# Sixteen modulation pieces multiplied in the loop over the Hyena filter jobs

## The chip, the cores and the metric

The kernel runs on one core of a Trainium2 chip. The metric is the device time of one execution in microseconds (us). TensorE (PE) multiplies matrices and loads weights beside that (PEld); VectorE (DVE), ScalarE (ACT) and GpSimd (POOL) compute on tiles; SyncE (SP) issues DMAs. Each engine works off its own instructions in order.

## The reference

A two-layer backbone over 1024 latent tokens of width 1024 and 256 context tokens. Layer 0 mixes tokens with a bidirectional RG-LRU (512 channels) and with an order-2 Hyena (512 channels); layer 1 is a convolution module; each layer ends in a mixture of 16 experts, and each sub-layer is modulated by a vector that depends on the conditioning `c`:

```python
def _adaln(cvec, w_mod, b_mod, n_chunks):
    m = jax.nn.silu(cvec) @ w_mod[:, :n_chunks * D_MODEL] + b_mod[:n_chunks * D_MODEL]
    return [m[:, None, j * D_MODEL:(j + 1) * D_MODEL] for j in range(n_chunks)]

# Hyena in layer 0: kf is the transform of learned filters
kf = _hyena_filters_fft(h.shape[1], p)
z = v
for o in range(HYENA_ORDER):
    z = gates[o] * _fftconv(z, kf[:, o], p['filt_bias'][o])
```

`w_mod` has 1024 x 6144 numbers for each of the two layers; everything is fp32.

## The kernel before, in words

**Modulation.** The product with `w_mod` is cut into pieces. A piece is 128 rows (index k, 0 to 7) by 2048 columns (a third s of a layer's 6144): `ada_load` (L224) takes a buffer of the pool `wr` (tag `w`, four buffers of 1 MB) and issues one 1 MB DMA on SP; `ada_mm` (L235) multiplies it by the conditioning in four matmuls of 128x512, each into its own 32 rows of one PSUM tile, which is held over the eight pieces of a third. After the eighth, `ada_end` copies the sums (L260, ACT), transposes them (L264, four, PE), adds the bias (DVE) and, for s of 1 and 2, transposes two results into rows (L284, PE) and stores them (L287, SP). `fill(n)` does n times: multiply the oldest loaded piece, then load another. 40 pieces are on the list: layer 0 with s = 0, 1, 2 and layer 1 with s = 0, 1. The last third of layer 1 comes later in the kernel and isn't touched.

**Filter stage, 0 to 128 us.** The eight pieces of s = 0 of layer 0 are multiplied at its start, since the norm of x needs them. Then `filters` does eight jobs (four blocks of 128 channels, two orders). A job makes its signal (L413 PE, L414 DVE) one job ahead, transforms it on PE (q0 L436, qa L440/L441, qb L445/L446, 128x128 matmuls), copies sums from PSUM (L455 to L457, ACT), combines them on DVE into K (L458 to L474) and stores K to memory (`kd`, L475, SP). K takes a buffer of the same pool `wr`. Between jobs `next(other)` advances the norm of x (L305 loads, L310, L326 transposes, L329).

**Projections and RG-LRU, 128 to 270 us.** `piece` loads 512 KB of `w_in` (`wst`, L715, SP), splits it into `wh` (L161, ACT) and the remainder `wlo` (L162, DVE), and `proj` multiplies in three passes (L156 to L158, PE, into P).

**Hyena, 270 to 550 us.** Four rounds i, one for each block of 128 channels, two orders each. A round: projection and short convolution of v (`short`, L786 to L788), transform on PE (`hy_fwd` L612, copies L615 on ACT), first step on DVE (`hy_st1` L622/L623), the transform's rest and the product with K on DVE (`hy_mid`, L584 to L640), inverse transform on PE (`hy_inv` L651), gate on DVE (`hy_gate` L659) and transposes back (`to_tok` L668). K is loaded again from `kd` into a buffer of `wr` (L606). In each round `fill(4)` stands before the first transform and again before the second gate's projection, 32 pieces in the four rounds.

**Order.** The program is written as above, and a scheduler then fixes the order of each engine's instructions; SP's DMAs stand in one order too, and one that waits holds up those behind it. So a call that is moved in the text moves others.

**After 550 us** come the output projection, the experts and layer 1.

Of the kernel before, what the change touches and what calls it, by code (L numbers as in the profile page):

```python
# [148 lines left out]
class Builder:  # L149
# [247 lines left out]
    def filters(self, fk, other):  # L397
        nc, A = self.nc, self.A
        V = nc.vector
        c = math.sqrt(0.5)  # L400
        G, Gn, h2, ws = self.G, self.Gn, self.h2, self.ws

        def signal(qd, o):
            cs = slice(qd * 128, qd * 128 + 128)
            if o == 0 and qd + 1 < 4:
                self.filt_win(fk, qd + 1)
            win = self.wins[qd]
            sd = fk.tile([128, 2, 8, 128], F32, name="sd", tag="sd", bufs=2)
            for i in range(2):
                for a in range(0, 8, 4):  # L410
                    q = self.ps.tile([128, 4, 128], F32, name="q", tag="n")
                    for j in range(4):
                        nc.tensor.matmul(q[:, j], h2[:, a + j], ws[:, o, i, cs], start=True, stop=True)  # L413
                    V.tensor_tensor(sd[:, i, a:a + 4], q, win[:, a:a + 4], op=OP.mult)  # L414
            V.tensor_tensor(sd[:1, 0, 0], sd[:1, 0, 0], sd[:1, 1, 0], op=OP.add)
            V.scalar_tensor_tensor(sd[:1, 0, 0], sd[:1, 0, 0], 0.5, self.fbias[:, o, cs], op0=OP.mult, op1=OP.add)
            return sd

        jobs = [(qd, o) for qd in range(4) for o in range(2)]
        sds = [signal(*jobs[0])]  # L420
        for n, (qd, o) in enumerate(jobs):
            sd = sds.pop(0)
            if 0 < n < 7:
                sds.append(signal(*jobs[n + 1]))
            if n:
                for _ in range(3):
                    next(other, None)
            K = self.wr.tile([128, 8, 2, 128], F32, name="w", tag="w")
            q0 = self.ps.tile([128, 2, 2, 128], F32, name="q0", tag="n")
            qa = self.ps.tile([128, 4, 2, 128], F32, name="qa", tag="w")  # L430
            qb = self.ps.tile([128, 4, 2, 128], F32, name="qb", tag="w")
            for i in range(2):
                mc = slice(i * 128, i * 128 + 128)
                oc = slice(128 - i * 128, 256 - i * 128)
                for j, a in enumerate((0, 4)):
                    nc.tensor.matmul(q0[:, j, i], G[:, a, mc], sd[:, i, a], start=True, stop=True)  # L436
            for a in range(1, 4):
                for i in range(2):
                    mc = slice(i * 128, i * 128 + 128)
                    nc.tensor.matmul(qa[:, a, i], G[:, a, mc], sd[:, i, a], start=True, stop=False)  # L440
                    nc.tensor.matmul(qa[:, a, i], G[:, 8 - a, mc], sd[:, i, 8 - a], start=False, stop=True)  # L441
            for a in range(1, 4):
                for i in range(2):
                    oc = slice(128 - i * 128, 256 - i * 128)
                    nc.tensor.matmul(qb[:, a, i], G[:, a, oc], sd[:, i, a], start=True, stop=False)  # L445
                    nc.tensor.matmul(qb[:, a, i], Gn[:, 3 - a, oc], sd[:, i, 8 - a], start=False, stop=True)  # L446
            if n == 0:
                sds.append(signal(*jobs[1]))
                for _ in range(3):
                    next(other, None)  # L450
            T = fk.tile([128, 10, 2, 128], F32, name="kT", tag="kT", bufs=1)
            r4, r1, r2, r3, i1, i2, e0, e4, f, g = (T[:, j] for j in range(10))
            CS = fk.tile([128, 2, 3, 2, 128], F32, name="kC", tag="kC", bufs=1)
            C, S = CS[:, 0], CS[:, 1]
            nc.scalar.copy(r4, q0[:, 1])  # L455
            nc.scalar.copy(T[:, 1:4], qa[:, 1:4])
            nc.scalar.copy(T[:, 4:6], qb[:, 1:3])  # L457
            V.tensor_tensor(e0, q0[:, 0], r4, op=OP.add)  # L458
            V.tensor_tensor(e4, q0[:, 0], r4, op=OP.subtract)
            V.tensor_tensor(f, r1, r3, op=OP.add)  # L460
            V.tensor_tensor(g, r1, r3, op=OP.subtract)
            V.tensor_tensor(C[:, 1], e0, r2, op=OP.subtract)
            V.tensor_tensor(e0, e0, r2, op=OP.add)
            V.tensor_tensor(K[:, 0], e0, f, op=OP.add)
            V.tensor_tensor(K[:, 4], e0, f, op=OP.subtract)
            V.scalar_tensor_tensor(C[:, 0], g, c, e4, op0=OP.mult, op1=OP.add)
            V.scalar_tensor_tensor(C[:, 2], g, -c, e4, op0=OP.mult, op1=OP.add)
            V.tensor_tensor(S[:, 1], i1, qb[:, 3], op=OP.subtract)
            V.tensor_tensor(f, i1, qb[:, 3], op=OP.add)
            V.scalar_tensor_tensor(S[:, 0], f, c, i2, op0=OP.mult, op1=OP.add)  # L470
            V.scalar_tensor_tensor(S[:, 2], f, c, i2, op0=OP.mult, op1=OP.subtract)
            for i, (pl, mi) in enumerate(((OP.add, OP.subtract), (OP.subtract, OP.add))):
                V.tensor_tensor(K[:, 1:4, i], C[:, :, i], S[:, :, i], op=pl)
                V.tensor_tensor(K[:, 7:4:-1, i], C[:, :, i], S[:, :, i], op=mi)  # L474
            nc.sync.dma_start(self.kd[o][qd], K)  # L475

# [126 lines left out]
    def hy_fwd(self, p, J):  # L603
        nc = self.nc
        J["K"] = K = self.wr.tile([128, 8, 2, 128], F32, name="w", tag="w")
        nc.sync.dma_start(K, self.kd[J["o"]][J["qd"]])  # L606
# [64 lines left out]
    def even_mixer(self, st, so):  # L671
        nc, tc, A = self.nc, self.tc, self.A

        def pool(st, name, side=None):
            return st.enter_context(tc.tile_pool(name=name, bufs=1, side=side, reuse_waits="tile"))
# [3 lines left out]
        with ExitStack() as s1, ExitStack() as sl:  # L679
# [4 lines left out]
            with ExitStack() as s2:  # L684
                pf = pool(s2, "fl", "right")
                with tc.tile_pool(name="fs", bufs=1, side="right", reuse_waits="tile") as fs:
                    self.filt_mlp(pf, fs)
                fk = pool(s2, "fk", "right")
                pn = pool(s2, "pn0", "right")
                for _ in range(4):  # L690
                    self.ada_load()
                self.filt_open(fk)
                for k in range(4):
                    self.ada_mm()
                    self.ada_load()

                def halves():
                    for k in range(4):
                        self.ada_mm()
                        if k % 2:  # L700
                            yield
                    rows = [self.norm_rows(pn, A["x"][0:512, :], 4, 6, True)]
                    yield
                    for i in range(2):
                        if i:
                            rows.append(self.norm_rows(pn, A["x"][512:1024, :], 4, 6, True))
                        yield from self.norm_steps(pn, rows[i], self.gg[0][0], self.mod[0], hh[i], hl[i], dve=False, hb=2)

                self.filters(fk, halves())
            wl = pool(sl, "wl")  # L710
            src = A["w_in"].rearrange("(k p) n -> p k n", p=128)

# [78 lines left out]
            def tok(y):  # L791
                ut = py.tile([128, 8, 128], F32, name="ut", tag="u", bufs=2)
                self.to_tok(y, ut)
                return ut
# [14 lines left out]
            for i in range(4):  # L809
                J0 = dict(o=0, qd=i, u=tok(short(i)))  # L810
                if i == 0:
                    with tc.issue_after(getattr(gload, "ins", gload)):
                        nc.sync.dma_start(self.IG, A["IG"])
                        self.fill(4)
                else:
                    self.fill(4)
                self.hy_fwd(py, J0)
                self.hy_st1(py, J0)
                if pend:
                    drain()  # L820
                self.hy_mid(py, J0)
                J0["gate"] = short(4 + i)
                self.fill(4)
                g1 = short(8 + i)
                pend.append(J0)
                J1 = dict(o=1, qd=i, u=drain(), gate=g1)
                self.hy_fwd(py, J1)
                self.hy_st1(py, J1)
                self.hy_mid(py, J1)
                pend.append(J1)  # L830
# [847 lines left out]
```

## Time and profile before

| | |
|---|---|
| median of 3 runs | 2288.9 us (2285.1 to 2289.81) |
| profiled execution | 2288.93 us, of which the span 2287.0 |
| mean granted TensorE clock | 0.962 |
| busy over the span | PE 2122.7 us (93%), PEld 1653.2 (72%), DVE 1819.6 (80%), ACT 1201.4 (53%) |
| the 320 instructions of L235 on PE | 43.8 us together |

The span is what the profile covers; times in the rows count from its start. A busy share is an average over stages of different kinds, so the rows below are taken by stage. In a row of the order of time, the bracket gives the engine's idle time before the row and the instruction that ended it; several equal instructions in a row stand as one with their count.

### The profile page before, as it was taken

To read this page: it belongs to the slowest core of one execution; us is meant where nothing else is said; L and a number is where in the kernel's file an instruction comes from. 1 tells how busy PE (TensorE), PEld (TensorE's weight loads), DVE (VectorE), ACT (ScalarE), POOL (GpSimd) and SP (SyncE) were. 2 spreads that over 40 slices of the span, in tenths; PEclk is the share of its full clock that TensorE was granted. 3 is DMA by queue.
4 is the path that set the end of the run, shared out by engine and by line. 5 is a ranking of instruction groups with operands and counts; after the bars stand their busy time and mean duration, and the time that the engine had idled before them with its cause. 6 is when DMAs were issued, how large, how long until landed. Compare 5 with 4: busy or idle time off the path is not lost. (4 is left out here: it accounts for less than half of the span.)

```text
span 2287.0 us, 28692 instructions
## 1 busy us (share of the span) xinstructions
PE 2122.7 (93%) x10626; PEld 1653.2 (72%) x10626; DVE 1819.6 (80%) x2877; ACT 1201.4 (53%) x1458; POOL 126.8 (6%) x128
## 2 busy tenths in 40 slices
PE   7999998988967999999999899979679999999997
PEld 5976766756745877878778588867457777777775
DVE  5879799997596989999888534276968898888887
ACT  3658621213214777777777521134247777676774
POOL 0000000000001000000000100010010000000001
PEclk9999998989988999999999899989889999999999
DMA  7241573654848999999998744334679999999974
GB/s 283 102 138 47 194 274 122 228 195 150 293 171 313 367 395 375 391 385 377 393 377 307 233 129 154 104 119 180 254 293 365 389 367 388 370 376 379 372 268 156
DMA packets 210021, 616.09 MB, mean 269 GB/s; under 512 B 27988, under 2 KB 76758, under 8 KB 200089
## 3 DMA queue, kind: packets, MB, share of 16 engines
q1 hardware_dynamic: 198610, 572.84, 66.3%
q0 software_dynamic: 11248, 41.42, 7.1%
q8 instruction: 83, 1.36, 0.2%
q14 instruction: 56, 0.46, 0.1%
q10 hardware_dynamic: 24, 0.01, 0.0%
HBM read 558.62 MB, written 55.61 MB: 269 GB/s over the span
## 5 line engine op out<-in xcount | busy, mean ns | idle before, releaser
L162 DVE TENSOR_TENSOR e<-wx,e 128x1024 fp32r<-128x1024 f32 x516 | 617.6, 1221 | 87.0 <-ACT e L161 74.0
L161 ACT CAST e<-wx 128x1024 fp32r<-128x1024 f32 x516 | 540.2, 1051 | 226.1 <-PE P L158 224.0
L156 PE MATMUL P<-e,th 128*128 128x512 f32 x1384 | 562.9, 407 | 0.0
L158 PE MATMUL P<-e,tl 128*128 128x512 f32 x1384 | 543.5, 393 | 0.8 <-DVE tl L162 0.8
L157 PE MATMUL P<-e,th 128*128 128x512 f32 x1384 | 543.2, 392 | 0.0
L157 PEld LDWEIGHTS P<-e,th 128*128 128x128 f32 x1384 | 260.3, 188 | 60.9 <-DVE e L162 3.8
L156 PEld LDWEIGHTS P<-e,th 128*128 128x128 f32 x1384 | 260.1, 188 | 60.8 <-issue 7.2
L158 PEld LDWEIGHTS P<-e,tl 128*128 128x128 f32 x1384 | 259.9, 188 | 60.0 <-DVE tl L162 1.2
L162 DVE TENSOR_TENSOR e<-w,e 128x1024 fp32r<-128x1024 f32 x176 | 211.6, 1222 | 49.6 <-ACT e L161 29.4
L156 PE MATMUL P<-hh,wh 128*128 128x512 f32 x576 | 229.8, 400 | 16.4 <-DVE y L788 12.9
L161 ACT CAST e<-w 128x1024 fp32r<-128x1024 f32 x176 | 183.9, 1051 | 93.4 <-PE P L158 74.5
L157 PE MATMUL P<-hl,wh 128*128 128x512 f32 x576 | 229.3, 398 | 0.0
L158 PE MATMUL P<-hh,wlo 128*128 128x512 f32 x576 | 228.3, 397 | 0.1
L156 PEld LDWEIGHTS P<-hh,wh 128*128 128x128 f32 x576 | 109.5, 190 | 50.2 <-issue 24.0
L157 PEld LDWEIGHTS P<-hl,wh 128*128 128x128 f32 x576 | 109.5, 190 | 26.6 <-issue 4.3
L158 PEld LDWEIGHTS P<-hh,wlo 128*128 128x128 f32 x576 | 109.1, 189 | 26.4 <-issue 4.0
L1314 POOL DMA_INDIRECT acc<-yo,ix x31 | 50.7, 1635 | 923.9 <-DVE yo L1313 923.9
L162 DVE TENSOR_TENSOR tl<-q,th 128x512 fp32r<-128x512 f32 x128 | 84.7, 683 | 5.3 <-ACT th L161 4.1
L161 ACT CAST wh<-w 128x1024 fp32r<-128x1024 f32 x16 | 16.7, 1049 | 124.1 <-PE P L157 110.4
L1274 PE MATMUL P<-wx,xf 128*128 128x512 f32 x176 | 79.1, 592 | 0.0
L161 ACT CAST th<-q 128x512 fp32r<-128x512 f32 x128 | 71.8, 587 | 1.7 <-PE q L1239 1.7
L297 POOL TENSOR_TENSOR rs<-ms,nh 128x1 f32<-128x1 f32 x42 | 23.9, 570 | 830.2 <-issue 436.2
(411 smaller groups left out, 3022.8 us busy)
## 6 DMA issues: line engine op xcount, KB each, us to landing
wx<-i_exp_w SPq DMA_DIRECT2D x272, 1024.0 KB, 8.2
w<-i_exp_w SPq DMA_DIRECT2D x96, 1024.0 KB, 7.7
w<-i_w_mod SPq DMA_DIRECT2D x40, 1024.0 KB, 7.8
wst<-i_w_in SPq DMA_DIRECT2D x20, 512.0 KB, 4.5
kd<-w SPq DMA_DIRECT2D x8, 1024.0 KB, 5.2
w<-kd SPq DMA_DIRECT2D x8, 1024.0 KB, 8.5
acc<-res SPq DMA_DIRECT2D x16, 512.0 KB, 3.0
e<-i_exp_w SPq DMA_DIRECT2D x16, 512.0 KB, 8.0
```

The lines of the kernel that those rows point to most:

```text
L156: t.matmul(o, lh, rh, start=start, stop=False)
L157: t.matmul(o, lh, rl, start=False, stop=False)
L158: t.matmul(o, ll, rh, start=False, stop=stop)
L161: self.nc.scalar.copy(hi, src)
L162: self.nc.vector.tensor_sub(lo, src, hi.bitcast(F32))
L297: nc.gpsimd.tensor_tensor(r, m, self.nh[:, :n], op=OP.pow)
L1274: nc.tensor.matmul(P[:, ns], f[:, k], h[:, ns], start=k == 0, stop=k == 7)
L1314: self.last = nc.gpsimd.indirect_dma_start(self.acc[l][:, :], bass.IndirectOffsetOnAxis(ap=xT[e][1][:, 0:1], axis=0), yo, None, compute_op ...
```

## The change

In the loop over the filter jobs, every job but the first gets two `fill(1)`, one before and one behind the buffers that the job takes; the first two of them get one more `ada_load`. What is loaded by the end of the loop is multiplied after it. These are the 16 pieces of layer 0 with s = 1 and 2: 13 in the loop and three after it, with two `ada_end`. In Hyena each `fill(4)` is a `fill(2)`, which leaves the 16 pieces of layer 1.

```diff
@@ filters, loop over the jobs @@
             if n:
                 for _ in range(3):
                     next(other, None)
+                self.fill(1)
+                if n < 3:
+                    self.ada_load()
             K = self.wr.tile([128, 8, 2, 128], F32, name="w", tag="w")
             q0 = self.ps.tile([128, 2, 2, 128], F32, name="q0", tag="n")
             qa = self.ps.tile([128, 4, 2, 128], F32, name="qa", tag="w")
             qb = self.ps.tile([128, 4, 2, 128], F32, name="qb", tag="w")
+            if n:
+                self.fill(1)
@@ caller @@
                 self.filters(fk, halves())
+                while self.ada_have:
+                    self.ada_mm()
@@ Hyena, round i @@
                     with tc.issue_after(getattr(gload, "ins", gload)):
                         nc.sync.dma_start(self.IG, A["IG"])
-                        self.fill(4)
+                        self.fill(2)
                 else:
-                    self.fill(4)
+                    self.fill(2)
                 self.hy_fwd(py, J0)
...
                 J0["gate"] = short(4 + i)
-                self.fill(4)
+                self.fill(2)
                 g1 = short(8 + i)
```

In the new file later lines are shifted: L436 is L441, L446 is L451, L475 is L480, L612 is L617, L651 is L656, L668 is L673, L715 is L722.

On SP, the end of the filter stage. `kd` are the stores of K (the numbers 71, 75, 72 and 76 are those of jobs 4 to 7), `wst` are blocks of w_in, `x<-i_ctx` the context rows, `w<-i_w_mod` pieces. Before:

```order
L475 DMA kd_71<-w 128x2048
L475 DMA kd_75<-w 128x2048
L715 DMA wst<-i_w_in 128x8x128 x2
L475 DMA kd_72<-w 128x2048
L305 DMA x<-i_ctx 128x1024 x2
L715 DMA wst<-i_w_in 128x8x128 x2
L475 DMA kd_76<-w 128x2048
```

And in the new program:

```order
L480 DMA kd_75<-w 128x2048
L224 DMA w<-i_w_mod 128x2048 x2
L480 DMA kd_72<-w 128x2048
L224 DMA w<-i_w_mod 128x2048
L722 DMA wst<-i_w_in 128x8x128
L480 DMA kd_76<-w 128x2048
L305 DMA x<-i_ctx 128x1024 x2
L287 DMA rowd_79<-w 8x2x128
L722 DMA wst<-i_w_in 128x8x128 x3
```

The first blocks of w_in stood ahead of the store kd_72 of job 6; the first now stands behind that store and a piece's load, and the second behind the store of job 7.

On PE, the last matmuls of the last filter job and the first of the projections (P). Before:

```order
L445 MATMUL qb<-sd,G 128x128
L446 MATMUL qb<-sd,Gn 128x128
L156 MATMUL P<-hh_152,wh 128x512
L157 MATMUL P<-hl_154,wh 128x512
L156 MATMUL P<-hh_152,wh 128x512
L157 MATMUL P<-hl_154,wh 128x512
L158 MATMUL P<-hh_152,wlo 128x512
```

And now:

```order
L450 MATMUL qb<-sd,G 128x128
L451 MATMUL qb<-sd,Gn 128x128
L235 MATMUL q<-w,sp 32x512 x12
L156 MATMUL P<-hh_152,wh 128x512
L157 MATMUL P<-hl_154,wh 128x512
L264 MATMUL t<-idn,w 128x128 x4
L158 MATMUL P<-hh_152,wlo 128x512
```

Three pieces (L235, four matmuls each) now stand between the job's last matmul and the first projection, and the four transposes that end a third stand among the projections.

On PE, the third round of Hyena, around the transform of its first order (`q<-ut`, L612, now L617). Before:

```order
L157 MATMUL P<-hl_155,wh 128x512
L158 MATMUL P<-hh_153,wlo 128x512
L284 MATMUL q<-idn,gg_144 8x128
L284 MATMUL q<-idn,mod_140 8x128
L235 MATMUL q<-w,sp 32x512 x12
L612 MATMUL q<-ut,G_2046 128x128 x16
L651 MATMUL q<-IG,pq 128x128 x16
L235 MATMUL q<-w,sp 32x512 x4
```

And now:

```order
L673 MATMUL q<-idn,y 128x128 x8
L264 MATMUL t<-idn,w 128x128 x4
L235 MATMUL q<-w,sp 32x512 x4
L617 MATMUL q<-ut,G_2171 128x128 x8
L158 MATMUL P<-hh_153,wlo 128x512
L156 MATMUL P<-hh_153,wh 128x512
L157 MATMUL P<-hl_155,wh 128x512
...
L158 MATMUL P<-hh_153,wlo 128x512
L235 MATMUL q<-w,sp 32x512 x8
L156 MATMUL P<-hh_152,wh 128x512
L617 MATMUL q<-ut,G_2171 128x128 x8
L656 MATMUL q<-IG,pq 128x128 x16
L157 MATMUL P<-hl_154,wh 128x512
```

Three pieces stood right before the whole transform; now one piece and half of the transform stand earlier, and two pieces before the other half.

## Rows read from the trace of the kernel before

**Rows 1.** The page: its span, and GB/s moved in 40 equal slices.
```profile
span 2287.0 us, 28692 instructions
...
GB/s 283 102 138 47 194 274 122 228 195 150 293 171 313 367 395 375 391 385 377 393 377 307 233 129 154 104 119 180 254 293 365 389 367 388 370 376 379 372 268 156
```

**Rows 2.** Stretch, length; busy PE, PEld, DVE, ACT, POOL; PE clock, DMA share, GB/s.
```profile
42.50:124.00 81.50, 76.96 (x657) 74.91 (x653) 70.43 (x179) 50.08 (x79) 4.75 (x8) 0.98 0.39 130
128.00:134.00 6.00, 6.00 (x14) 4.36 (x15) 5.27 (x10) 2.30 (x4) 0.55 (x1) 0.50 1.00 333
128.00:270.00 142.00, 139.33 (x593) 104.57 (x594) 114.19 (x129) 109.82 (x130) 1.10 (x2) 0.98 0.25 83
280.90:356.50 75.60, 75.18 (x445) 51.14 (x444) 71.11 (x134) 13.67 (x24) 0.00 (x0) 1.00 0.73 271
377.00:490.60 113.60, 113.14 (x674) 85.53 (x673) 106.16 (x196) 22.09 (x36) 0.00 (x0) 1.00 0.56 205
```

**Rows 3.** TensorE in order of time: start us, us, line, operation, [idle before].
```profile
38.97 3.64 PE L235 MATMUL q<-w,sp 128*32 128x512 f32 x32
...
86.96 1.97 PE L326 MATMUL q<-idn,x 128*128 128x128 f32 x8 [0.87 <-ACT h L329]
...
112.00 0.60 PE L326 MATMUL q<-idn,x 128*128 128x128 f32 x4
...
115.12 0.39 PE L446 MATMUL qb<-sd,Gn 128*128 128x128 f32 x2
...
121.20 0.46 PE L445 MATMUL qb<-sd,G 128*128 128x128 f32 x2 [1.93 <-DVE kT L469]
...
128.00 0.76 PE L156 MATMUL P<-hh,wh 128*128 128x512 f32 x1 [3.29 <-DVE kT L469]
```

**Rows 4.** TensorE's waits, 42.5 to 134 us: total, times, longest.
```profile
PE q L326 <- ACT x L310: 1.6, 4, 0.6
```

**Rows 5.** SP's DMA issues in order of time.
```profile
115.25 1.65 SPq L715 DMA_DIRECT2D wst<-i_w_in  x2
```

**Rows 6.** ScalarE in order of time.
```profile
115.54 0.59 ACT L457 COPY kT<-qb 128x512 f32<-128x512 f32 x1 [0.64 <-PE qb L446]
...
121.91 1.05 ACT L161 CAST wh<-wst 128x1024 fp32r<-128x1024 f32 x1 [5.78 <-DMA wst<-i_w_in]
```

**Rows 7.** VectorE in order of time, jobs 6 and 7 of the filters.
```profile
120.32 0.40 DVE L468 TENSOR_TENSOR kC<-kT,qb 128x256 f32<-128x256 f32 x1
...
123.30 0.55 DVE L474 TENSOR_TENSOR w<-kC 128x384 f32<-128x384 f32 x1
...
127.78 1.22 DVE L162 TENSOR_TENSOR wlo<-wst,wh 128x1024 fp32r<-128x1024 f32 x1
```

**Rows 8.** VectorE in order of time, Hyena.
```profile
283.89 0.42 DVE L622 TENSOR_TENSOR pq<-q,y 128x256 f32<-128x256 f32 x1 [1.37 <-ACT y L615]
...
415.15 0.42 DVE L622 TENSOR_TENSOR pq<-q,y 128x256 f32<-128x256 f32 x1 [2.54 <-ACT y L615]
```

**Rows 9.** VectorE's waits, 274 to 560 us.
```profile
DVE zt L659 <- PE q L651: 3.9, 4, 1.3
```

**Rows 10.** TensorE in order of time, Hyena.
```profile
281.70 1.07 PE L235 MATMUL q<-w,sp 128*32 128x512 f32 x8
...
344.25 3.84 PE L651 MATMUL q<-IG,pq 128*128 128x128 f32 x32
...
368.69 2.07 PE L651 MATMUL q<-IG,pq 128*128 128x128 f32 x8 [2.52 <-DVE pq L586]
...
372.72 4.72 PE L651 MATMUL q<-IG,pq 128*128 128x128 f32 x24 [1.95 <-DVE pq L600]
...
410.79 2.78 PE L235 MATMUL q<-w,sp 128*32 128x512 f32 x24
```

**Rows 11.** The page's DMA issues: count, KB each, median us to landing.
```profile
w<-i_w_mod SPq DMA_DIRECT2D x40, 1024.0 KB, 7.8
...
kd<-w SPq DMA_DIRECT2D x8, 1024.0 KB, 5.2
```

## The prediction

> **What bounds the kernel now.** I read the stages first (busy time by stretch), then TensorE's order of time at the stage ends, then who releases it. From 42.5 to 124 us, the loop over the filter jobs, PE is busy 76.96 of 81.50 us and its weight loads 74.91, DVE 70.43 [rows 2]: PE is the engine that has no room. The projections and the RG-LRU after it are PE too, 139.33 of 142.00 us, so whatever is late at their start is late at their end. The Hyena stage is the odd one. In its two long stretches, 280.9 to 356.5 and 377 to 490.6, PE reads as busy 75.18 of 75.60 and 113.14 of 113.60 us, but DVE also has 71.11 and 106.16 us of work there [rows 2]. DVE can't give these up, since the change takes no DVE work out worth naming. So PE time taken out of these stretches comes back only as far as DVE waits there for PE: 4.5 + 7.4 = 11.9 us at the very most. Everything after 550 us is the same work with the same buffers; I let it move with its start.
>
> The profiled execution took 2288.93 us, 1.9 more than its span of 2287.0 [rows 1], and the median of the runs shown is 2288.9. So a shift in the span is added to 2288.9.
>
> **The price of a piece.** A modulation piece is four matmuls in the code and eight instructions of 128x512 in the trace (x32 for four pieces). Four pieces in a row, at 38.97, took 3.64 us [rows 3], so 0.91 each; one alone, at 281.70, took 1.07 [rows 10], its end in part under the next. I take 0.93. Sixteen pieces are 14.9 us, and their two endings (six transposes each, some 0.55) bring it to 16.0. All of it goes from Hyena into the stage ahead of 128 us. No engine does less.
>
> **What the filter stage pays.** (1) Up to the last qb matmuls of job 6, which end at 115.5 us now [rows 3], the new order puts 11 pieces and one ending: 11 x 0.93 + 0.55 = 10.8 us. Before, PE idled there from 42.54 on for 1.6 us on ACT's x [rows 4] and 0.87 us at 86.96, where eight transposes then ran cold in 1.97 us, some 0.8 too long against 0.60 for four at 112.00 [rows 3]. If pieces fill all of this, job 6's qb ends at 115.5 + 10.8 - 3.3 = 123.0; if none, at 126.3. Pieces stand near all three places, but each also waits for its own load, so I take 123.5.
>
> (2) The end of the stage is a chain over SP, and this is where the price is set. Now the first block of w_in is issued at 115.25 [rows 5], ahead of job 6's store, and its cast runs at 121.91 [rows 6]; w_in's remainder wlo stands inside job 7's work on DVE at 127.78 [rows 7], and PE runs on at 128.00. In the new order of SP that block stands behind job 6's store and behind the load of the sixteenth piece. K of job 6 needs from the end of qb the copy of 0.59 [rows 6] and DVE's row from 120.32 to 123.85, 3.5 us [rows 7]: 123.5 + 4.1 = 127.6. Then store, piece and block, 2.5 MB, go out in one train. For a train of this kind the trace has two blocks and a store, 2 MB, from 115.25 to the cast at 121.91: 6.66 us, so 8.3 for 2.5 MB: 135.9. Cast 1.05 and wlo 1.22: 138.2. Against 128.00 that is **10.2 us late**. The last three pieces (2.8 us) and the old waits of 1.93 us at 121.20 and 3.29 us at 128.00 [rows 3] all lie under this chain; they cost nothing while it is the later, and the pieces alone would set a shift of 16.0 less all that idle. PE waits before the projections then as now, and starts them at half clock as now: 0.50 from 128 to 134 [rows 2], so no difference.
>
> Bounds of this term: with every wait filled and the projections warm, 16.0 - 1.6 - 0.87 - 0.8 - 1.93 - 3.29 - 3.0 (half of the 6.00 us at 0.50) = +4.5. With no wait filled before job 6 ends, 126.3 instead of 123.5: +13.0. I take +10.2, nearer the upper, since the train on SP is in the program's order and not a matter of pace. The loads themselves, 16 MB more, are some 200 GB/s on top of 130 over the loop's 81.50 us [rows 2]; the sum stays under the 390 that slices of the page reach later [rows 1], so I cost them at nothing but their place in the queue.
>
> **What Hyena gives back.** Only DVE's waits that a piece on PE caused. At 283.89 DVE waited 1.37 us behind the first transform, which a piece at 281.70 splits in two [rows 8, 10]; the new order doesn't split it: 1.0. At 415.15, 2.54 us, after three pieces in a row from 410.79 to 413.50 ahead of the transform [rows 8, 10]; in the new order half of that transform stands some twenty projections earlier and two pieces stand before the other half: 1.8. For the inverse transform DVE waited four times, 3.9 us in all [rows 9]; pieces stand before it in some of these places and with half as many I take somewhat over half, 2.2. Sum 5.0 us. Bounds: 1.8 (only the triple) and 11.9 (DVE without any wait). The stretches between, where PE waits for DVE, give nothing.
>
> For which engine binds, the Trainium skill ("Perfetto Trace Analysis", Identifying the Most-Contended Engine) would have TensorE judged by the busy share of its weight loads, because busy matmuls mislead when they are pipelined. The trace agrees in direction: 74.91 of 81.50 (92%) in the filter loop, 51.14 of 75.60 (68%) and 85.53 of 113.60 (75%) in Hyena [rows 2]. By it alone the pieces leave a place with room for one without, nothing comes back, and the time would be 2288.9 + 10.2 = 2299.1.
>
> **Sum.** +10.2 - 5.0 = +5.2: **2294.1 us**. About 0.2% (4.6 us) is what a measurement of this kernel can tell from no change, so the forecast stands on that edge.
>
> **Rivals.**
> A. Hyena is bound by PE, and the change makes the kernel faster. For it: PE reads solid in both stretches [rows 2]. Then 14.9 us come back and 10.2 are paid: 2284.2. Against it: DVE has no 14.9 us to give there, 11.9 at most, which with +10.2 makes 2287.2; it needs a cheaper filter term as well (with +7, 2284).
> B. The pieces hide in the filter stage: waits, cold stretches and the half-clock start take them up, and the block of w_in isn't the last to come. +4.5 to +5.5, and 5.0 back: 2289. For it: the idle time is there [rows 3, 4]. Against: SP's order.
> C. The clock makes it worse, far past the forecast. Where PE waits between transforms, it loses its clock: eight inverse transforms after 2.52 us of idle took 2.07 and the other 24 took 4.72, 6.79 against 3.84 for 32 at full clock [rows 10], 2.95 us. Pieces fill such gaps now. If two more places of the two long stretches fall to 1.2 GHz, with DVE waiting on them, 5.9 us: 2300.0. It decides where a piece that goes had left PE less idle than at 368.69. A sentence of the Trainium skill ("TensorE: Matmul & The Clock Gate", Why this matters for your kernels) warns against idle gaps between bursts of matmuls for this reason; these rows agree.
> D. Waits within the filter loop. The pieces share four buffers with the jobs' K: the ninth piece's load waits until a store has landed, 5.2 us after its issue in the median, and then takes 7.8 [rows 11]; with every SP load behind it in line (x rows, win). 13 us exceed a job's some 10, so PE stands 3 us before that piece, and once more at the eleventh, which stands behind it: +6 more, 2300.1.
>
> **Chances.** Forecast 0.45, A 0.15, B 0.18, C 0.11, D 0.11. Faster is A and a little of B: 0.16. B, the rest of A and the lower half of the forecast are within 0.2%: 0.39. Slower is the upper half with C and D: 0.45. The range 2283 to 2301 holds A's and D's times and leaves out the ends of the bounds; the forecast's own, with each term moved by half of its distance to its bounds, is 2290 to 2298.
>
> **What would show it.** First block of w_in issued after job 6's store near 127, and the projections going on between 136 and 140: the filter term. If they run before 134, B; after 141, D, with PE waits on w_mod in the loop. The RG-LRU stage keeps its length. Hyena's end is some 4 to 6 us later than 550 and DVE's wait near 415 has shrunk to under 1: the second term; if DVE's busy share there goes over 0.98, A; if new stretches of half clock stand in the two stretches, C. The forecast is wrong above all if DVE's gaps shrink by more than the pieces that stood before them, since the order of all engines around them is new.

## The result, and the profile after

The changed kernel took 2303.47 us (median of 4 runs, 2301.75 to 2305.45); the kernel before took 2288.43 beside it. The ratio is 1.0061, with a 95% interval of 1.0049 to 1.0073: 15 us slower, where 5.2 slower was forecast. It lies beyond the range (2283 to 2301).

The span grew by 15.3 us, from 2287.0 to 2302.3. Four landmarks on TensorE say where (us from the span's start; the last column is the span):

| kernel | job 6's last qb ends | projections go on | Hyena's first transpose | output projection | span |
|---|---|---|---|---|---|
| before | 115.5 | 128.0 | 269.7 | 552.4 | 2287.0 |
| after | 131.2 | 146.95 | 291.55 | 568.4 | 2302.3 |
| difference | +15.7 | +18.95 | +21.9 | +16.05 | +15.3 |
| forecast | +8.0 | +10.2 | +10.2 | +5.2 | +5.2 |

So the filter stage costs 18.95 us and not 10.2; the RG-LRU stage, thought unchanged, adds 2.9; Hyena gives back 5.8 (5.0 was forecast); what follows gives 0.75. The border between the last two stages is a choice: counted to Hyena's first transform (279.27 before, 300.13 after) the RG-LRU stage adds 1.9 and Hyena gives back 4.8.

Two stretches of the kernel after, the filter loop and Hyena, as [rows 2] (length; busy PE, PEld, DVE, ACT, POOL; granted clock, DMA share, GB/s), and Hyena before:

```profile
43.70:131.20 87.50, 85.38 (x688) 69.49 (x690) 66.64 (x168) 48.00 (x75) 4.81 (x8) 1.00 0.73 269
291.50:568.40 276.90, 230.98 (x1298) 184.80 (x1297) 252.92 (x441) 55.71 (x81) 0.00 (x0) 0.91 0.42 149
```

```profile
269.70:552.40 282.70, 249.48 (x1431) 186.08 (x1431) 254.56 (x445) 55.85 (x84) 0.00 (x0) 0.94 0.58 212
```

The first row runs to the end of job 6's qb. Of its 87.5 us PE is busy 85.38: nearly every us of the longer stage is work on PE, not a wait. The pieces alone, in the same stretch (L235; PE busy and count, PEld busy and count):

```profile
43.70:131.10 87.40, 15.67 (x88) 2.36 (x88) 1.00 0.73 269
```

88 instructions are the 11 pieces that I had counted, but they take 15.67 us and not 10.2. TensorE's order of time shows why, at one piece that the new order divides:

```profile
94.30 1.04 PE L235 MATMUL q<-w,sp 128*32 128x512 f32 x2
95.28 1.18 PE L326 MATMUL q<-idn,x 128*128 128x128 f32 x6
96.39 1.06 PE L235 MATMUL q<-w,sp 128*32 128x512 f32 x6
97.38 0.49 PE L446 MATMUL qa<-sd,G 128*128 128x128 f32 x2
```

Two instructions (the first of the piece's four matmuls) take 1.04 us; the other six take 1.06; eight in one go took 1.07 [rows 10]. PE pays about 0.98 us for a visit to a piece, however many of its four matmuls it does there. The scheduler divided the pieces at four places, so that 15 visits stand for 11 pieces.

The end of the stage went in the order that the prediction had, from a later start. On SP and ScalarE (beside [rows 5] and [rows 6]), and on PE:

```profile
136.29 0.33 SPq L480 DMA_DIRECT2D kd<-w  x1
137.13 0.33 SPq L224 DMA_DIRECT2D w<-i_w_mod  x1
137.53 1.24 SPq L722 DMA_DIRECT2D wst<-i_w_in  x1
```

```profile
145.85 1.04 ACT L161 CAST wh<-wst 128x1024 fp32r<-128x1024 f32 x1 [5.74 <-DMA wst<-i_w_in]
```

```profile
144.25 1.06 PE L235 MATMUL q<-w,sp 128*32 128x512 f32 x8 [2.90 <-DMA w<-i_w_mod]
146.95 0.80 PE L156 MATMUL P<-hh,wh 128*128 128x512 f32 x1 [1.64 <-ACT wh L161]
```

Store, sixteenth piece and first block of w_in go out in a row; PE waits for the piece's load and then for the block. From the store's issue to the cast are 9.6 us; I had 8.3.

In Hyena, VectorE's waits ahead of the first step and of the gate (before, beside [rows 9], and after), and PE's waits ahead of projections (before and after):

```profile
DVE pq L622 <- ACT y L615: 17.7, 7, 6.6
```

```profile
DVE pq L627 <- ACT y L620: 10.0, 9, 3.0
DVE zt L664 <- PE q L656: 5.1, 6, 1.3
```

```profile
PE P L156 <- DVE y L788: 12.9, 4, 4.0
```

```profile
PE P L156 <- DVE y L795: 25.4, 4, 9.3
```

PE loses 18.5 us of work there and the stage only 5.8: the rest became PE waiting for DVE, 25.4 us ahead of four projections where it had been 12.9. The 5.8 us are DVE's: it is idle for 24.0 us of the stage instead of 28.1, and has 1.6 us less to do (252.92 instead of 254.56). Its waits ahead of the first step shrank; the 6.6 us among the 17.7 are the one at Hyena's start, which now stands ahead of the first convolution, so 11.1 us should be compared with 8.2 (10.0 less 1.8 at the start). Waits for the inverse transform did not shrink (5.1 us in six, 3.9 in four in [rows 9]).

### The profile page after: what moved, and what is told of

Its sections match the earlier page's. It is cut to its first block, busy times and chain, and to the rows that moved or that the text cites. A ratio compares the mean times of both kernels' runs of the same rounds, so it can differ in the third digit from the quotient of the medians.

```text
span 2302.3 us, 28690 instructions
## 1 busy us (share of the span) xinstructions
PE 2123.9 (92%) x10626; PEld 1655.4 (72%) x10626; DVE 1821.1 (79%) x2877; ACT 1203.1 (52%) x1458; POOL 126.7 (6%) x128
## 5 line engine op out<-in xcount | busy, mean ns | idle before, releaser
L156 PE MATMUL P<-hh,wh 128*128 128x512 f32 x576 | 230.3, 401 | 28.1 <-DVE y L795 25.4
```

The costliest lines, as they stand in the source:

```text
L156: t.matmul(o, lh, rh, start=start, stop=False)
```

## The experiments

All ratios are to the kernel before on the same chip. Profiles begin the filter stage at different times (its first transposes of L264 start between 40.4 and 46.4 us), so within it I compare from there (43.53 before and 43.69 after, which leaves the landmarks above as they are).

**The two halves apart.** Hyena multiplies 32 pieces again, 16 of them twice.

```diff
+        self.ada_todo += [(1, s_, k) for s_ in range(2) for k in range(8)]
-                self.fill(2)
+                self.fill(4)   # all three in Hyena
```

> Filter stage as in the changed kernel, but Hyena multiplies 32 pieces again as before (the 16 of layer 1 twice, the second time over the same results). It splits the change into its two halves. Theory: the filter half costs some 19 us to the first projections and about 3 more in the RG-LRU stage, and Hyena's lighter load gives back 5.9; so this kernel is 5.9 us slower than the changed one: 2309.4, with the projections starting near 147 us. Rival (Hyena bound by TensorE, some other stage gives the rest): 15 us slower than the changed one, 2318. Rival (Hyena gives back nothing): 2303.5.

2310.17 us, 1.0097 (1.0082 to 1.0112): 6.7 slower than the changed kernel. Projections started at 146.4; the filter loop began 3.3 us earlier here and took 2.7 us longer, at a granted clock of 0.96 from 40 to 127 us (1.00 in the changed kernel). From Hyena's first transpose to the output projection are 283.7 us, where the changed kernel has 276.9 and the kernel before 282.7. So the lighter Hyena is worth some 7 us, not 15 and not nothing.

**Pieces kept whole.**

```diff
         for j in range(4):
-            self.nc.tensor.matmul(self.ada_q[...], sp, w[...], ...)
+            with self.tc.high_priority(offset=300 if j else 0):
+                self.nc.tensor.matmul(self.ada_q[...], sp, w[...], ...)
```

> The changed kernel, with the four matmuls of a piece kept next to each other on TensorE (the second to fourth get priority); nothing else is edited. Theory: TensorE pays 0.98 us for each visit to a piece, whether it does one of its four matmuls or all four, and 15 visits stood for 11 pieces before job 6's last transform; with 11 visits that transform ends 3.9 us earlier, at 127.2 instead of 131.1, the projections start near 143, and the time is 2299.6. Rival (the loads are what slows the filter stage, 16 MB more in it): the loads are the same, so no change, 2303.5 and 131.

2299.0 us, 1.0045 (1.0032 to 1.0058), 4.5 less than the changed kernel. Its pieces, and its whole PE work, up to the end of job 6's qb:

```profile
43.70:126.70 83.00, 11.51 (x88) 1.84 (x88) 1.00 0.75 280
```

```profile
43.70:126.80 83.10, 81.01 (x688) 68.93 (x690) 66.40 (x168) 47.78 (x75) 4.81 (x8) 1.00 0.75 279
```

The same 88 and 688 instructions, the same loads at 279 GB/s: PE's work falls by 4.37 us, the pieces' part by 4.16, and job 6's qb ends at 126.8. The projections start at 142.5 (143 was expected). The loads weren't the cause, the visits were; and the time, 2299.0, lies within the range that the prediction gave.

**No load ahead of the block of w_in.** On e3_whole, fourteen pieces in the filter stage: job 7's fills only multiply, and Hyena's first round takes the other two (not shown here).

```diff
-                self.fill(1)
+                self.fill(1) if n < 7 else self.ada_mm()   # both places in the loop
```

> As e3_whole, with the last two pieces left to Hyena (14 in the filter stage, 18 in Hyena), so that no piece's load stands between job 6's store and the first block of w_in on SP, and that block goes out ahead of the store. Theory: the chain of store, sixteenth piece and block sets the start of the projections; without it they start after job 7's K at about 137 to 138 instead of 143, and the block's order in the RG-LRU stage is nearer to before: 2293 to 2295. Rival (only TensorE's load counts there): two visits less, 2 us earlier than e3_whole: 2297.6, projections at 141.

2296.83 us, 1.0039 (1.0025 to 1.0052). The block goes out before job 6's work is done, and PE doesn't wait for it:

```profile
127.09 1.50 SPq L723 DMA_DIRECT2D wst<-i_w_in  x2
133.57 0.34 SPq L481 DMA_DIRECT2D kd<-w  x1
```

```profile
137.04 1.06 PE L236 MATMUL q<-w,sp 128*32 128x512 f32 x8
138.03 0.50 PE L156 MATMUL P<-hh,wh 128*128 128x512 f32 x1
```

From the first transposes (45.39) to the projections are 92.6 us, where e3_whole (43.71, 142.49) has 98.8. Of these 6.2 us, 4.4 are e3_whole's two waits for the chain over SP (2.76 for the sixteenth piece, 1.61 for the block), which are gone; the rest is the two pieces' own work. The RG-LRU stage had its old length too (140.6 from there to Hyena's first transpose, against 144.05 in e3_whole). But only 2 us came through to the end: PE's new order put the rest of the next projections before Hyena's first transform, which started at 292.95, 2.2 earlier than in e3_whole.

**The two other pieces later in Hyena.** On e4_fourteen.

```diff
-                        self.fill(3)   # before the first transform
+                        self.fill(2)
-                self.fill(3 if i == 0 else 2)
+                self.fill(3 if i < 2 else 2)
```

> As e4_fourteen, but the two pieces more in Hyena stand in the second halves of its first two rounds and not before its first transform. In e4_fourteen the projections started 4.5 us earlier than in e3_whole, yet the first transform only 2.2, since the order of TensorE put some 25 projections and an ending between. Theory (DVE starts its chain with that transform, so its start sets Hyena's end): the transform comes 3 to 5 us earlier, 2292 to 2294. Rival (DVE's start doesn't matter, the pieces' number does): 2296.8 as e4_fourteen.

2296.77 us, 1.0033 (1.0020 to 1.0046). The first transform started at 284.1, 8.8 earlier, and the output projection at 563.6, 2 later than in e4_fourteen. (In this profile the filter loop ran at a mean clock of 0.94, 4 us longer; its run took 2300.96, against the median of 2296.77.) So an earlier start of DVE's chain alone didn't bring the end forward; that theory fell.

**The order of the w_in splits.** On e3_whole, first one split on DVE moved forward, then all of them.

```diff
-                    self.split(wh, wlo, w)
+                    with tc.high_priority(offset=60):   # 300 in e13_wlo_all
+                        self.split(wh, wlo, w)
```

> As e3_whole, with a small priority for the split of the w_in blocks; on TensorE the order stays that of e3_whole, on DVE one remainder (wlo), that of the block before Hyena's first, moves ahead of the last convolutions of the RG-LRU stage, where it stood in the kernel before. Theory: the changed kernel has this wlo later, so the next block of w_in finds its buffer free 12 us later and TensorE waits some 3 us for it at the end of that stage; here the stretch from the first projection to the first Hyena transpose goes from 144.0 back to some 141, and the time is 2296.2. Rival (the stage is longer for another reason, as the transposes and rows that end a third, or the loads): 144 as in e3_whole, 2299.0.

> As e3_whole, with a strong priority for every split of a w_in block, so that each buffer comes free as early as it can (e6_wlo moved one split alone, and the RG-LRU stage took 148.8 us from the first projection to the first Hyena transpose, where e3_whole takes 144.0 and the kernel before 141.7). Theory (the splits' place on DVE and ACT makes the stage 3 us longer in the changed kernel, through late loads of w_in): the stretch goes to 140 to 142 and the time to 2296. Rival (splits ahead of the scan's work on DVE make the scan late, whatever the loads do): 144 or longer, 2299 or more.

e6_wlo: 2302.72, 1.0061 (1.0048 to 1.0074), against the expectation. The remainder stood earlier, but PE then waited 6.9 us for the next one, and the stretch was 148.8 us. e13_wlo_all: 2298.7, 1.0047 (1.0035 to 1.0059); stretch 143.1, between the two that were expected, and nothing in the time. With the splits elsewhere this stage is 4.8 us longer or 1.0 shorter than e3_whole's, but that their place makes the changed kernel's 2.9 us is not shown; this stays open.

**Whole pieces in the kernel before; pieces near PE's gaps.** The edit of e3_whole on the kernel before, and with it the second `fill(4)` of a round moved behind `hy_mid(py, J1)`.

> The kernel before, with the four matmuls of a piece kept next to each other; the four pieces that Hyena splits become whole. Theory (Hyena waits for DVE, and TensorE's time comes back only in DVE's few waits): 0 to 1.5 us faster, 2287 to 2288.5. Rival (Hyena is bound by TensorE): 3.9 us faster, 2284.5.

> No piece in the filter loop: the kernel before, with pieces whole, and the second four of each Hyena round placed after the round's last step of DVE, so that three pieces move from places ahead of DVE's work to right before the stretches where TensorE idles (356 to 377 us and 490 to 511 us before). Theory (DVE is the bound of Hyena, and it waits little for these pieces): 1 to 3 us faster than before, 2286 to 2288. Rival (TensorE's total in Hyena sets the end, and its place doesn't matter): no change, 2288.7.

2288.6 us, 0.9999 (0.9991 to 1.0008), and 2288.21, 0.9995 (0.9987 to 1.0004): no change, twice. In Hyena PE's work fell from 249.48 to 245.65 us with whole pieces, and the stage kept its length (282.70 before, 282.80). The same 0.98 us a visit that cost 4.5 us in the filter loop is worth nothing in Hyena. For f1_gaps the 1 to 3 us that I had expected weren't there.

**Half of the change.**

```diff
-                if n < 3:
+                if n < 2:
                     self.ada_load()
-            if n:
-                self.fill(1)   # the second one of a job
-                self.fill(2)
+                self.fill(3)   # all three in Hyena; pieces whole
```

> Half of the change: 8 pieces whole in the filter stage (one for each job but the first, one after it), 24 in Hyena with three for each fill. The first block of w_in goes out ahead of job 6's store. Theory: 8 visits of 1 us less some 3 us of the old waits, and no train on SP at the end: the projections start 5 us later than before (near 133), the RG-LRU stage keeps its length of before, Hyena gives 2.5 to 3 back: 2291. Rival (the cost goes by the number of pieces, half of 2299.0 - 2288.8): 2294.

2281.46 us, 0.9970 (0.9959 to 0.9980): faster than before by 7 us, where 2 slower was expected. The projections go on at 127.85, Hyena's first transpose is at 268.7, and its last inverse transform starts at 539.4, all within 1 us of before. Five of the eight stand ahead of job 6's last qb, which ends at 119.4, 3.9 us later than before; the waits of 1.93 and 3.29 us behind it [rows 3] are gone, and PE runs at a granted clock of 1.00 from 127.8 to 133.8, where it began the projections at 0.50 [rows 2]. Then the output projection starts at 544.15 and not at 552.36. The two last gate projections of the RG-LRU, which stand behind the Hyena loop in the program, come earlier there. ScalarE, before and then here (cast of yc, for which the output projection waits):

```profile
551.37 0.94 ACT L161 CAST th<-yc 128x896 fp32r<-128x896 f32 x1 [7.51 <-DMA yc<-ycd]
```

```profile
534.49 0.94 ACT L161 CAST th<-yc 128x896 fp32r<-128x896 f32 x1 [3.61 <-DMA yc<-ycd]
```

**The gates alone.** In the kernel before with whole pieces, in e3_whole and in e8_eight, the gates were written into earlier rounds.

```diff
-            for ct in (2, 3):
-                gate(py, ct, "cv", D)
...
                 self.hy_st1(py, J1)
+                if i in (1, 2):
+                    gate(py, i + 1, "cv", D)
```

> The kernel before with pieces whole and one edit far from the filter loop: the two last gate projections of the RG-LRU (512 KB of w_in, 48 matmuls, Gelu, product and a store each), which stand after the Hyena loop, are written into its second and third round. e8_eight, with 8 pieces in the filter loop, came out at 2281.5; its projections started when they did before and Hyena ended when it did before, but the output projection started 4.7 us after the last inverse transform and not 12.0, since the gates had come before it. Theory (e8 gained by this order of the gates and not by the place of the pieces): this kernel gains the same without any piece in the filter loop, 2281 to 2283. Rival (the pieces' place gave it): 2288.5.

> e3_whole (16 pieces in the filter stage, whole) with the gates written into Hyena's second and third round as in e9_gates_before. Theory: the same 7 us at Hyena's end, and the filter stage's loss stays: 2292, still slower than before. Rival (the gates move only where Hyena has 24 or more pieces, or fill what the pieces left): no change from e3_whole, 2299.0.

> e8_eight with the gates written into the second and third round as well. Theory: the gates were early there already, so no second gain: 2280 to 2283. Rival (earlier gates take TensorE's waits in Hyena's two gaps as well): 2276 to 2278.

2297.54 (1.0040, 1.0027 to 1.0053), 2308.8 (1.0085, 1.0072 to 1.0098) and 2289.35 (0.9999, 0.9990 to 1.0008): each 8 to 10 us slower than without the edit, and outside what was expected for any of them. In the first the wait at the end was gone (the output projection started 4.9 us after the last inverse transform, 12.0 before), but that transform came 15 us later. Then, in the kernel before with whole pieces, both gates in the last round, one before and one after its second transform, about where e8_eight has them:

> The kernel before with pieces whole; the two gate projections stand in Hyena's last round, one before and one after the first transform of its second order, about where e8_eight has them (e9_gates_before had them two rounds too early, and Hyena itself got 19 us longer there). Theory (what e8 gained is the wait for yc at Hyena's end, and goes with the gates' place alone): Hyena's inverse transform ends when it did before, the output projection starts 5 us after it and not 12, 2281 to 2283. Rival (the gates fit there only because a lighter Hyena leaves TensorE time for them): the second order is later by the two gates' 21 us of TensorE work less its waits, and the time is 2288 or more.

2293.98, 1.0022 (1.0013 to 1.0031). Again the wait shrank (4.8 us) and the last inverse transform was later, by 10 us. So the theory that the gates' place alone gave the 7 us fell. Its rival, that they fit there only because a lighter Hyena leaves PE the time, fits these runs, but no run holds the gates behind the loop with 8 pieces moved, so it isn't shown by itself. One trace bears on it: in e13_wlo_all, with 16 pieces moved, the gates come early as well (their Gelus at 520.37 and 539.64, the last inverse transform at 557.85, the output projection at 563.06). From Hyena's first transpose to the output projection it takes 276.0 us, e3_whole with late gates 277.1, e8_eight 275.4, and the kernel before 282.7. So with 16 pieces moved the gates' place is worth some 1 us, and Hyena with its end gives back about as much for 8 pieces (7.3 us) as for 16 (5.6 and 6.7): what differs is what the filter stage takes.

## Why the prediction was wrong

The direction was right and so was the order of the stage's end, but the filter stage cost 18.95 us and not 10.2. The 8.75 us between are 7.7 up to job 6's last qb, 2.3 in the chain over SP, and 1.2 less behind it. By the prediction's own steps:

- **The price of a piece** is the step that failed. "I take 0.93", times 11, was read from places where a piece stands whole. The new order divides four places, and a divided piece costs a visit more: 15.67 us and not 10.2 in the profile, 11.51 with whole pieces (1.05 each, since few stand in a row). The trace of before had the row that shows it, in Hyena:

```profile
305.57 1.04 PE L235 MATMUL q<-w,sp 128*32 128x512 f32 x2
306.54 1.16 PE L651 MATMUL q<-IG,pq 128*128 128x128 f32 x8
307.63 1.06 PE L235 MATMUL q<-w,sp 128*32 128x512 f32 x6
```

- **"If pieces fill all of this"**: they filled little. Of 2.5 us of waits in the loop 0.8 stayed, and 1.2 came new ahead of the signals (L413), so 2.0 were left; the cold stretch went. With whole pieces job 6's qb ends at 126.8, just past the bound of 126.3 for no wait filled, while I took 123.5. Of the 7.7 us by which that end was late against the forecast, the visits are 4.4, and the rest is this and the price of whole pieces.
- **The chain over SP** was right: store, sixteenth piece, block, cast, in that order. It took 1 us more on each side of the store's issue (5.1 instead of 4.1, 9.6 instead of 8.3). The train that the 8.3 was scaled from began with its store at 114.88, 0.37 us earlier than the prediction has it. "Cast 1.05 and wlo 1.22" was 1.2 too much: the first projection waits for the cast alone (the row at 146.95). PE's waits for this chain are 4.4 us in e3_whole, and e4_fourteen has none of them. "The last three pieces lie under this chain" was right, also of the two of job 7 that the sum left out: PE still waits behind them, 2.90 and 1.64 us.
- **"All of it moves with its start"**: the RG-LRU stage got 2.9 us longer. In the new order the blocks of w_in at its end are issued at 268.66 and 282.54, where the shift alone would give 263.6 and 270.8, and PE waits 3 us for their parts. The cause isn't settled. I had left this stage out of the range altogether.
- **What Hyena gives back**: 5.8 us measured (6.7 between e1_hyena32 and the changed kernel), 5.0 forecast. The reason was right: DVE has 252.92 us of work in 276.90, and the other PE time became waits. Two of the three places were right: DVE's wait at 283.89 went from 1.37 to 0.18 us (at 303.56), and the one at 415.15 from 2.54 to 0.79 (at 429.53), 1.2 and 1.8 us where I took 1.0 and 1.8. The third was wrong: the waits at the inverse transform, for which I took 2.2 us, grew by 1.2. DVE's work, put at nothing, fell by 1.6. That the sum came so near is partly luck. "A. Hyena is bound by PE" is refuted for this change by e1_hyena32, and for the last few us of PE time by b_whole.
- **"B. The pieces hide in the filter stage"** is false for 16 pieces and true for 8.
- **"C. The clock"**: the mean granted clock of Hyena fell from 0.94 to 0.91, and PE's waits at 378.17 and 510.30 us grew to 9.26, but DVE is busy all through them, and the places at half clock are those of before (0.50 from 382.8 to 390.5, and from 365.0 to 372.7 before). Eight inverse transforms took 2.08 us there, as before (2.07). The other 24 took 5.26 and 5.49 (4.72 and 4.33 before), and DVE waited up to 1 us more for the second; the last 28 of the stage took 3.39 (4.96 before). So it cost little, and gave as much elsewhere. Nor was it the 2.52 us of idle time that lost the clock in the row at 368.69 [rows 10]: it was at 0.50 from 365 on, behind a wait of 3.96 us.
- **"D. Waits within the filter loop"**: no wait on a piece's load in the loop; the only one, 2.90 us, is the sixteenth's.

The page's rule that I weighed (the Trainium skill, "Perfetto Trace Analysis", Identifying the Most-Contended Engine) pointed the right way: PE's weight loads had little room in the filter loop and much in Hyena. The sum of 2299.1 by it, with nothing given back, was nearer to the time, but for a wrong reason, since Hyena did give 5.8.

## What to carry to other kernels

Price a group of matmuls that run side by side in column tiles by visits, not by instructions, and count the visits in the new order: here a row with one or three matmuls of a group of four cost as much as the group. Work that is moved into a stage whose engine is busy 94% is free only as far as it fills that engine's waits, and it gives back only the waits that it caused where it stood. The dose can matter more than the idea: 16 pieces cost 15 us, and 8 of them, kept whole and with no load ahead of the next stage's first block, gained 7, since the filter stage took nothing for them and Hyena gave back about as much for 8 as for 16. Count also which DMA stands last at the stage's end.

## What the runs showed of the hardware that was not expected

Two instructions of 128x512 into 32 columns (one matmul of a piece) held TensorE for 1.04 us at 94.30, and all eight of a piece into four column groups for 1.07 [rows 10]; without other edits, keeping them together took 4.16 us off 15.67 for 88 instructions. The loads beside it didn't slow PE: with DMA at 0.75 and 279 GB/s it ran at a granted clock of 1.00 in e3_whole, and its 600 other instructions took 69.5 us (81.01 less 11.51), where before 592 took 69.39 from 43.5 to 115.5 at 118 GB/s.
